# Gate-and-up chunks of a two-layer hybrid block: all four sums in one bank pool, read halfway by ScalarE, with other buffers and other priorities

## The chip, the cores and the metric

The kernel runs on one core of one Trainium2 chip. The metric is the device time of one execution in microseconds (us); lower is better. A time is the median of several runs of the same compiled program. Beside these runs stands one execution taken by the hardware profiler, and all rows shown below come from it.

## The reference, cut to what matters

Two layers run over 256 tokens of width 2048, all in float32. Each layer has a mixer (a state-space part and a latent attention), a cross-attention to 256 memory rows, and a feed-forward part. The change bears most on the last of these, and on what lies just before it:

```python
for l in range(DEPTH):                                   # DEPTH = 2
    ...
    x = x + mixed                                        # mixer, then @ w_out[l]
    ...
    x = x + memory_cross_attention(h, m, ...)            # ends in @ w_xo[l]
    h = rms_norm(x, ffn_norm_g[l])
    x = x + swiglu(h, w_gate[l], w_up[l], w_down[l])

def swiglu(h, w_gate, w_up, w_down):                     # w_gate, w_up: 2048 x 5632; w_down: 5632 x 2048
    return (jax.nn.silu(h @ w_gate) * (h @ w_up)) @ w_down
```

## The kernel before, in words

**Products in three parts.** A float32 product is made of three products of the rounded type float32r. Each unit of weights (256 rows by 512 columns, 512 KB, named `raw`) is split into `hi` (a cast, on ScalarE, ACT in the rows) and `lo` (raw minus hi, on VectorE, DVE). TensorE (PE) then multiplies hi by both parts of the activations and lo by the upper part. So every unit costs one cast on ACT, one subtraction on DVE and 6 matmuls (12 where both halves of the tokens take it).

**The feed-forward part.** The 5632 hidden columns go in 11 chunks of 512. Chunk 0 is done plainly. Chunks 1 to 10 go through `gate_up`, a seven-product scheme after Strassen for three quarters of the 2048 rows, with plain products (`x1`) for the rest. For it, `seven_rows` makes once per layer the split blocks a11, a12, a22, a21 of x and four sums s1 to s4 of them (the tiles `x7`, whose sums lie in `xs`; in the rows their splits are named `x<-xg,x` for a and `x<-xs,x` for s). The weights are summed on the fly by `add` on DVE (rows `raw<-raw,raw`): per chunk b11, b12, b22, b21 are pairs of 256-row units, and h11, h12, h22, h21 are single units that belong to the half blocks. Four sums are gathered in PSUM banks: `q`, `f` (from the pool acc, 4 banks) and `cg`, `cu` (from the pool tp, 4 banks). `q` is read three times while it goes on growing. The results meet in `uu` and `gg`; `gg` is then turned by a DMA transpose (`turn`: halves `hs`, turned `ht`, both in b4) and split into hTh and hTl for the down product. Chunks go in sections [0], [1,2], [3,4] and so on. After each chunk of a section come half of the four column blocks of the down product of the section before (`down`, each adds its two banks to x by `add_x`), so after chunks 1 and 2 it is 48 matmuls each, and after the later ones 96.

**What sets the order.** The program is first recorded and then put in order by a planner (`Recorder.issue`). It gives each engine, again and again, the operation that can start first by the planner's own costs, and of several with the same start the one with the lowest priority number: the place in the record plus `rec.bias`. `split_w` records its splits with -400, `add` its sums with -425, everything else in the feed-forward part with 0. The order on every engine and on the DMA queue of SyncE (SP) is then fixed, and each engine works through its own in that order.

**Buffers.** `b4` has 22 buffers of 4 KB per partition, `w` has 20 (raw, hi and lo of all weights), `s2` has 6 of 2 KB, acc and tp have 4 banks each. An operation that needs a buffer while `ahead` tiles recorded before it are still without one may take it only if more than min(margin, ahead) buffers are free; the margins stand in the last call of the kernel: b4 6, s2 2, tp 0, w 99, acc 4. `load_unit` asks for weights up to three units ahead, in the order of the list `ahead`.

Of the kernel before, what the change touches and what calls it, by code (L numbers as in the profile page):

```python
# [8 lines left out]
F32 = mybir.dt.float32  # L9
# [8 lines left out]
P = 128  # L18
S = 256
# [358 lines left out]
def hybrid_kernel(ctx: ExitStack, tc: tile.TileContext, const, vec, rows, x_in, x_tr, mem, mem_tr, positions, w_in, w_q_b,  # L378
# [110 lines left out]
    def load_unit(w, r0, c0, n, pieces=1):  # L489

        if not ahead and not asked:
            return ask(w, r0, c0, n, pieces)
        key = id(w), r0, c0
        while key not in asked or (ahead and len(asked) <= 2):
            first = ahead.pop(0)
            asked[id(first[0]), first[1], first[2]] = ask(*first, 512)
        return asked.pop(key)

    def load_raw(w, r0, c0, n, pieces=1):

        return [load_unit(w, r0 + 256 * h, c0, n, pieces) for h in range(2)]

    def ask(w, r0, c0, n, pieces=1):
        raw = wpool.tile([P, 2, n], F32, tag="w", name=nm("raw"), bufs=20)
        src = w[r0:r0 + 256, c0:c0 + n].rearrange("(k p) n -> p k n", p=P)
        for i in range(pieces):
            k = slice(2 // pieces * i, 2 // pieces * (i + 1))
            SP.dma_start(raw[:, k, :], src[:, k, :])
        return raw
# [116 lines left out]
    def norm_chunk_whole(j, ssx, g, by_dma=False):  # L626

        x_squares(j, ssx)
        xg = b4([P, 4, S], "xg")
        if by_dma:  # L630
            turn(lambda t: x[j][:, t, :], xg.rearrange("p b s -> p (b s)"))
            for b in range(4):
                copy(xg[:, b, :], xg[:, b, :], g[:, 4 * j + b:4 * j + b + 1])
            return xg
        for pair in range(2):
            ps = tp_tile().rearrange("p (b s) -> p b s", b=2)
            for i in range(2):
                b = 2 * pair + i
                for t in range(NT):
                    T.transpose(ps[:, i, t * P:(t + 1) * P], x[j][:, t, b * P:(b + 1) * P], ident)  # L640
                copy(xg[:, b, :], ps[:, i, :], g[:, 4 * j + b:4 * j + b + 1])
        return xg

    def seven_rows(xa, xb, n):


        a = {f"a{t + 1}{i + 1}": src[:, :, t * P:(t + 1) * P] for i, src in enumerate((xa, xb)) for t in range(NT)}
        if n == 4:
            sums = [b4([P, 2, 4, P], "xs") for _ in range(2)]
            tmp = [sums[i // 2][:, i % 2] for i in range(4)]  # L650
        else:
            sums = b4([P, 4, 2, P], "xs")
            tmp = [sums[:, i] for i in range(4)]
        out, room = {}, []
        for name in ("a11", "a12", "a22", "a21", "s1", "s2", "s3", "s4"):
            if name[0] == "s":
                a[name] = tmp[int(name[1]) - 1]
                do, u, v = {"s1": (V.tensor_sub, "a21", "a22"), "s2": (V.tensor_sub, "s1", "a11"),
                            "s3": (V.tensor_sub, "a11", "a21"), "s4": (V.tensor_add, "a12", "s2")}[name]
                do(a[name], a[u], a[v])  # L660
            if n == 4:
                d = b4([P, 2, 4, P], "x7", F32R)
            else:
                if not room:
                    both = b4([P, 2, 2, 2, P], "x7", F32R)
                    room = [both[:, 0], both[:, 1]]
                d = room.pop(0)
            copy(d[:, 0], a[name])
            V.tensor_sub(d[:, 1], a[name], d[:, 0].bitcast(F32))
            out[name] = d  # L670
        return out

    def load_T(src, j, g, name, pieces=1):
# [486 lines left out]
    def mem_T(l):  # L1160
# [10 lines left out]
        rec.after = None  # L1171
        return mT

    def add_x(j, accs):
        for t in range(NT):
            xs = x[j][:, t, :]
            V.tensor_add(xs, xs, accs[t])

    mixer_end, hidden_end = [None], [None]

# [120 lines left out]
            src = w[r0 + 256 * h:r0 + 256 * (h + 1), c0:c0 + 512].rearrange("(k p) n -> p k n", p=P)  # L1301
            G.dma_start(raw[h], src, accum_op=ALU.add)

    def add(out, a, b, do=V.tensor_add):
        rec.bias -= 425
        for o, u, v in zip(out, a, b) if isinstance(out, list) else [(out, a, b)]:
            do(o, u, v)
        rec.bias += 425

    def gate_up(wg, wu, c, x1, half, full, rstd):  # L1310

        c0 = 512 * c
        q, f = acc_tile(), acc_tile()
        cg, cu = tp_tile(), tp_tile()
        gg, uu = b4([P, NT, 512], "gg"), [s2([P, 512], "uu") for _ in range(NT)]  # L1320

        def product(acc, d, raw, start=False, stop=False):
            parts = split_w(raw)
            order = [(h, k, i) for h in range(len(parts)) for k, i in ((0, 1), (1, 1), (0, 0), (0, 2), (1, 0), (1, 2))]
            for m, (h, k, i) in enumerate(order):
                T.matmul(acc, d[:, i // 2, 2 * h + k, :], parts[h][i % 2][:, k, :], start=start and m == 0,
                         stop=stop and m == len(order) - 1, skip_group_check=True)

        b11 = load_raw(wg, 1024, c0, 512)
        product(q, full["a11"], b11, start=True)  # L1330
        h11 = load_unit(wg, 0, c0, 512)
        product(q, half["a11"], [h11])
        A.copy(gg[:, 0, :], q)

        b12 = load_raw(wu, 1024, c0, 512)
        add(b11, b11, b12)
        product(f, full["s1"], b11, start=True)
        h12 = load_unit(wu, 0, c0, 512)
        add(h11, h11, h12)
        product(f, half["s1"], [h11])  # L1340
        A.copy(uu[0], f)

        b22 = load_raw(wu, 1536, c0, 512)
        add(b11, b11, b22)
        add(b12, b12, b22)
        product(cu, full["s4"], b22, start=True)
        h22 = load_unit(wu, 256, c0, 512)
        add(h11, h11, h22)
        add(h12, h12, h22)
        product(cu, half["s4"], [h22])  # L1350
        product(q, full["s2"], b11)
        plus(b11, wg, 1536, c0)
        product(q, half["s2"], [h11])
        add(uu[0], uu[0], q, V.tensor_sub)

        b21 = load_raw(wg, 1536, c0, 512)
        product(cg, full["a12"], b21, start=True)
        h21 = load_unit(wg, 256, c0, 512)
        add(h11, h11, h21)
        product(cg, half["a12"], [h21])  # L1360
        product(q, full["s3"], b12)
        product(q, half["s3"], [h12])
        mm_chunk([cu, f], x1, load_w(wu, 512, c0, 512), 512, [False] * NT, [True, True], again=True)
        A.copy(uu[1], f)
        add(uu[1], uu[1], q, V.tensor_sub)
        add(uu[0], uu[0], cu)
        mm_chunk([cg, q], x1, load_w(wg, 512, c0, 512), 512, [False] * NT, [True, False], again=True)
        add(gg[:, 0, :], gg[:, 0, :], cg)
        A.activation(gg[:, 0, :], gg[:, 0, :], AF.Silu, scale=rstd[:, 0:1])

        product(q, full["a22"], b11)
        product(q, half["a22"], [h11], stop=True)
        A.activation(gg[:, 1, :], q, AF.Silu, scale=rstd[:, 1:2])
        for t in range(NT):
            V.scalar_tensor_tensor(gg[:, t, :], uu[t], rstd[:, t:t + 1], gg[:, t, :], op0=ALU.mult, op1=ALU.mult)
        return gg

    def ffn(l, xT, rstd):
# [19 lines left out]
        for sec in sections:  # L1398
            for i, c in enumerate(sec):
                if c == 0:  # L1400
                    ahead.extend((w, r + h, 0) for w in (wg, wu) for r in FULL for h in (0, 256))
                else:
                    ahead.extend((w, r, 512 * c) for w, r in (
                        (wg, 1024), (wg, 1280), (wg, 0), (wu, 1024), (wu, 1280), (wu, 0), (wu, 1536), (wu, 1792),
                        (wu, 256), (wg, 1536), (wg, 1792), (wg, 256), (wu, 512), (wu, 768), (wg, 512), (wg, 768)))
                if before:
                    n = DC // len(sec)
                    ahead.extend((wd, 512 * r + h, 512 * j) for j in range(n * i, n * (i + 1)) for r in before
                                 for h in (0, 256))
# [3 lines left out]
        for sec in sections:  # L1413
            hT = []
            for i, c in enumerate(sec):
                if c == 0:
                    xs = [lambda i, k, t: half[f"a{t + 1}{1 + k // 2}"][:, i, k % 2, :], x1]
                    xs += [lambda i, k, t, b=b: full[f"a{t + 1}{b}"][:, i, k, :] for b in (1, 2)]
                    ag = gemm(xs, wg, FULL, 0, 512)
                    hh = b4([P, NT, 512], "gg")  # L1420
                    for t in range(NT):
                        A.activation(hh[:, t, :], ag[t], AF.Silu, scale=rstd[:, t:t + 1])
                    au = gemm(xs, wu, FULL, 0, 512)
                    for t in range(NT):
                        V.scalar_tensor_tensor(hh[:, t, :], au[t], rstd[:, t:t + 1], hh[:, t, :], op0=ALU.mult,
                                               op1=ALU.mult)
                else:
                    hh = gate_up(wg, wu, c, x1, half, full, rstd)
                hc = chunk_T("hT")
                split_T_dma(hc, lambda t: hh[:, t, :], None, hh.rearrange("p t (u s) -> p (t u) s", s=S), (A, V))  # L1430
                hT.append(hc)
                if before:
                    n = DC // len(sec)
# [88 lines left out]
```

## Time and profile before

| | |
|---|---|
| median of 3 runs | 2263.99 us (2261.82 to 2264.88) |
| profiled execution, device time | 2267.05 us |
| its span, first to last instruction | 2265.3 us |
| mean granted TensorE clock | 0.997 of full speed |
| PE busy, share of the span | 98% |
| DVE busy | 84% |
| ACT busy | 66% |
| DMA, mean rate | 215 GB/s |

The profiled execution is 3.06 us longer than the median of the runs, and 1.75 us of its time lie outside the span. Matmuls follow one another in a pipeline, so a busy PE need not be a PE at its peak; the gaps of PE are what a change of order can win, since the number of matmuls stays.

### The profile page before, as it was taken

To read this page: it belongs to the slowest core of one execution; us is meant where nothing else is said; L and a number is where in the kernel's file an instruction comes from. 1 tells how busy PE (TensorE), PEld (TensorE's weight loads), DVE (VectorE), ACT (ScalarE), POOL (GpSimd) and SP (SyncE) were. 2 spreads that over 40 slices of the span, in tenths; PEclk is the share of its full clock that TensorE was granted. 3 is DMA by queue.
4 is the path that set the end of the run, shared out by engine and by line. 5 is a ranking of instruction groups with operands and counts; after the bars stand their busy time and mean duration, and the time that the engine had idled before them with its cause. 6 is when DMAs were issued, how large, how long until landed. Compare 5 with 4: busy or idle time off the path is not lost.

```text
span 2265.3 us, 29133 instructions
## 1 busy us (share of the span) xinstructions
PE 2222.9 (98%) x10118; PEld 1845.7 (81%) x10118; DVE 1910.6 (84%) x2568; ACT 1500.4 (66%) x2183; POOL 93.0 (4%) x78
## 2 busy tenths in 40 slices
PE   9999999998999999999999999999989999999999
PEld 9878878787888888888898788887878888888787
DVE  7898876789998999999778888857899999999894
ACT  7768666766766666676666686657666667666762
POOL 0001000000000000000000010000000000000000
PEclk9999999999999999999999999999999999999999
DMA  9866496676777777787777665856767777777773
GB/s 319 236 193 186 142 284 196 187 212 197 239 224 212 229 232 235 228 247 226 194 230 223 172 177 171 244 185 182 219 201 226 232 220 213 236 231 226 239 234 138
DMA packets 374515, 487.96 MB, mean 215 GB/s; under 512 B 145376, under 2 KB 168544, under 8 KB 374368
## 3 DMA queue, kind: packets, MB, share of 16 engines
q1 hardware_dynamic: 363456, 465.13, 65.1%
q0 software_dynamic: 10912, 20.98, 5.5%
q8 instruction: 79, 1.29, 0.2%
q14 instruction: 68, 0.56, 0.1%
HBM read 450.92 MB, written 2.10 MB: 200 GB/s over the span
## 4 chain that ended last, share of the span: by engine, by line
PE 71%; DVE 6%; DMA 5%; issue 2%; ACT 1%; SPq 0%; DVEq 0%; ACTq 0%
PE acc L374 59%; PE tp L374 13%; DVE lo L374 3%; DMA raw<-in_w_up_dram 1%; DVE raw L374 1%; DMA ht<-hs 1%; ACT hi L374 1%; DVE x L374 1%; DMA raw<-in_w_xv_dram 0%; DMA raw<-in_w_out_dram 0%; DMA raw<-in_w_in_dram 0%; DVE uu L374 0%; DMA raw<-in_w_gate_dram 0%; SPq L374 0%; DVE hTl L374 0%
## 5 line engine op out<-in xcount | busy, mean ns | idle before, releaser
L374 ACT CAST hi<-raw 128x1024 fp32r<-128x1024 f32 (+3 forms) x996 | 1002.7, 1034 | 559.9 <-PE acc L374 223.4
L374 DVE TENSOR_TENSOR lo<-raw,hi 128x1024 fp32r<-128x1024 f32 (+3 forms) x998 | 1167.9, 1200 | 177.3 <-ACT hi L374 125.2
L374 PE MATMUL acc<-hi,x 128*128 128x512 f32 x1392 | 373.1, 392 | 0.0
L374 PEld LDWEIGHTS acc<-hi,x 128*128 128x128 f32 x1392 | 263.4, 189 | 55.4
L374 PE MATMUL acc<-hi,xTh 128*128 128x512 f32 (+1 forms) x768 | 289.3, 377 | 0.0
L374 PE MATMUL acc<-hi,xTl 128*128 128x512 f32 (+1 forms) x768 | 289.1, 376 | 0.0
L374 DVE TENSOR_TENSOR raw<-raw,raw 128x1024 f32<-128x1024 f32 x200 | 239.2, 1221 | 50.7 <-DMA raw<-in_w_up_dram 50.2
L374 PE MATMUL acc<-hi,hTh 128*128 128x512 f32 x704 | 273.9, 389 | 0.0
L374 PE MATMUL acc<-hi,hTl 128*128 128x512 f32 x704 | 273.9, 389 | 0.0
L374 PE MATMUL acc<-lo,x 128*128 128x512 f32 x696 | 214.8, 394 | 13.2 <-DVE x L374 13.2
L374 PE MATMUL acc<-lo,xTh 128*128 128x512 f32 (+1 forms) x768 | 211.7, 378 | 6.0 <-DVE uu L374 4.2
L374 PE MATMUL acc<-lo,hTh 128*128 128x512 f32 x704 | 191.2, 390 | 1.3 <-DVE lo L374 1.3
L374 PEld LDWEIGHTS acc<-lo,xTh 128*128 128x128 f32 x768 | 140.6, 188 | 31.3 <-DVE uu L374 6.8
L374 PEld LDWEIGHTS acc<-lo,x 128*128 128x128 f32 x696 | 131.1, 190 | 42.5 <-DVE x L374 14.9
L374 PEld LDWEIGHTS acc<-hi,xTh 128*128 128x128 f32 x768 | 144.8, 189 | 23.2 <-issue 0.7
L374 PEld LDWEIGHTS acc<-hi,xTl 128*128 128x128 f32 x768 | 144.7, 188 | 23.1 <-issue 0.7
L374 PEld LDWEIGHTS acc<-lo,hTh 128*128 128x128 f32 x704 | 131.8, 188 | 30.1 <-DVE lo L374 3.0
L374 PEld LDWEIGHTS acc<-hi,hTh 128*128 128x128 f32 x704 | 132.1, 188 | 27.5
L374 PEld LDWEIGHTS acc<-hi,hTl 128*128 128x128 f32 x704 | 132.1, 188 | 27.4
L374 PE MATMUL tp<-hi,x 128*128 128x512 f32 x480 | 128.6, 390 | 0.0
L374 DVE TENSOR_TENSOR x<-x,acc 128x512 f32<-128x512 f32 x128 | 83.5, 682 | 32.5 <-PE acc L374 32.4
L374 PEld LDWEIGHTS tp<-hi,x 128*128 128x128 f32 x480 | 90.1, 188 | 19.2
(306 smaller groups left out, 2781.7 us busy)
## 6 DMA issues: line engine op xcount, KB each, us to landing
raw<-in_w_gate_dram SPq DMA_DIRECT2D x176, 512.0 KB, 4.9
raw<-in_w_up_dram SPq DMA_DIRECT2D x176, 512.0 KB, 4.5
raw<-in_w_down_dram SPq DMA_DIRECT2D x176, 512.0 KB, 5.4
raw<-in_w_in_dram SPq DMA_DIRECT2D x80, 512.0 KB, 4.4
raw<-in_w_out_dram SPq DMA_DIRECT2D x64, 512.0 KB, 4.5
raw<-in_w_gate_dram POOLq DMA_DIRECT2D x40, 512.0 KB, 7.5
raw<-in_w_in_dram SPq DMA_DIRECT2D x46, 368.0 KB, 4.5
raw<-in_w_kv_b_dram SPq DMA_DIRECT2D x16, 512.0 KB, 3.9
```

The costliest lines, as they stand in the source:

```text
L374: fn(*args, **kw)
```

## The change

It has these parts.

1. In `gate_up` the four sums q, f, cg, cu all come from tp; acc is left to the plain products and `down`.
2. ACT copies `q` to uu where it copied `f` before, and DVE subtracts that copy from `f`, where it subtracted `q` in its bank from a copy of `f`. For the second row block the copy of q now stands ahead of the plain product into cu and f.
3. `gg` and the chunk-0 `hh` are two half tiles in s2 in place of one b4 tile; the turned rows get a b4 tile of their own (`whole`).
4. From chunk 1 on, h11 and h12 (the units with row 0 in the list) are loaded to b4 in place of w.
5. The products of b22 and h22 into cu are recorded ahead of the sums that use b22 and h22.
6. In `seven_rows` the four sums s1 to s4 and their splits are recorded with 300 added.
7. `add_x` goes through `add`, so it has -425 in all its places.
8. In `norm_chunk_whole` the four transposes of a pair stand ahead of the two scaled copies out of their bank.

```diff
     def load_unit(w, r0, c0, n, pieces=1):
...
-            asked[id(first[0]), first[1], first[2]] = ask(*first, 512)
+            asked[id(first[0]), first[1], first[2]] = ask(*first[:3], 512, 1, first[3:])
...
-    def ask(w, r0, c0, n, pieces=1):
-        raw = wpool.tile([P, 2, n], F32, tag="w", name=nm("raw"), bufs=20)
+    def ask(w, r0, c0, n, pieces=1, other=False):
+        raw = b4([P, 2, n], "raw") if other else wpool.tile([P, 2, n], F32, tag="w", name=nm("raw"), bufs=20)
...
                     T.transpose(ps[:, i, t * P:(t + 1) * P], x[j][:, t, b * P:(b + 1) * P], ident)
+            for i in range(2):
+                b = 2 * pair + i
                 copy(xg[:, b, :], ps[:, i, :], g[:, 4 * j + b:4 * j + b + 1])
...
         for name in ("a11", "a12", "a22", "a21", "s1", "s2", "s3", "s4"):
+            if name == "s1":
+                rec.bias += 300
...
+        rec.bias -= 300
         return out
...
+    def add(out, a, b, do=V.tensor_add):
+        rec.bias -= 425
+        for o, u, v in zip(out, a, b) if isinstance(out, list) else [(out, a, b)]:
+            do(o, u, v)
+        rec.bias += 425
+
     def add_x(j, accs):
         for t in range(NT):
             xs = x[j][:, t, :]
-            V.tensor_add(xs, xs, accs[t])
+            add(xs, xs, accs[t])
...
-        q, f = acc_tile(), acc_tile()
-        cg, cu = tp_tile(), tp_tile()
-        gg, uu = b4([P, NT, 512], "gg"), [s2([P, 512], "uu") for _ in range(NT)]
+        q, f, cg, cu = (tp_tile() for _ in range(4))
+        gg, uu = [[s2([P, 512], n) for _ in range(NT)] for n in ("gg", "uu")]
...
         product(f, half["s1"], [h11])
-        A.copy(uu[0], f)
 
         b22 = load_raw(wu, 1536, c0, 512)
+        product(cu, full["s4"], b22, start=True)
         add(b11, b11, b22)
         add(b12, b12, b22)
-        product(cu, full["s4"], b22, start=True)
         h22 = load_unit(wu, 256, c0, 512)
+        product(cu, half["s4"], [h22])
         add(h11, h11, h22)
         add(h12, h12, h22)
-        product(cu, half["s4"], [h22])
         product(q, full["s2"], b11)
         plus(b11, wg, 1536, c0)
         product(q, half["s2"], [h11])
-        add(uu[0], uu[0], q, V.tensor_sub)
+        A.copy(uu[0], q)
+        add(uu[0], f, uu[0], V.tensor_sub)
...
         product(q, half["s3"], [h12])
+        A.copy(uu[1], q)
         mm_chunk([cu, f], x1, load_w(wu, 512, c0, 512), 512, [False] * NT, [True, True], again=True)
-        A.copy(uu[1], f)
-        add(uu[1], uu[1], q, V.tensor_sub)
+        add(uu[1], f, uu[1], V.tensor_sub)
         add(uu[0], uu[0], cu)
         mm_chunk([cg, q], x1, load_w(wg, 512, c0, 512), 512, [False] * NT, [True, False], again=True)
...
-                    ahead.extend((w, r, 512 * c) for w, r in (
+                    ahead.extend((w, r, 512 * c) + ((1,) if r == 0 else ()) for w, r in (
...
-                split_T_dma(hc, lambda t: hh[:, t, :], None, hh.rearrange("p t (u s) -> p (t u) s", s=S), (A, V))
+                split_T_dma(hc, lambda t: hh[t], None, None, (A, V))
```

## Rows read from the trace of the kernel before

**Rows 1.** The page's first part: busy time, share of the span, instructions.
```profile
PE   2222.9 (98%) x10118; PEld 1845.7 (81%) x10118; DVE 1910.6 (84%) x2568; ACT 1500.4 (66%) x2183; POOL 93.0 (4%) x78
```

**Rows 2.** Waits of PE, whole span: in total, times, longest (us).
```profile
PE acc L374 <- DVE x L374: 13.2, 4, 5.7
PE tp L374 <- DVE x L374: 5.2, 4, 2.3
PE tp L374 <- DVE lo L374: 4.8, 7, 1.2
PE acc L374 <- DVE uu L374: 4.2, 6, 1.3
PE acc L374 <- DVE lo L374: 3.1, 4, 1.8
```

**Rows 3.** Windows around chunk 2's start, both layers: busy (instructions); clock, DMA share, GB/s.
```profile
519.00:531.00 12.00, 12.00 (x55) 9.94 (x54) 11.00 (x11) 4.60 (x5) 0.00 (x0) 1.00 0.57 187
531.00:543.00 12.00, 6.36 (x17) 4.69 (x16) 8.14 (x11) 4.27 (x6) 0.00 (x0) 0.72 0.37 92
...
1658.00:1670.00 12.00, 6.29 (x19) 4.72 (x18) 8.49 (x12) 4.53 (x7) 0.00 (x0) 0.72 0.35 93
```

**Rows 4.** Timeline of DVE and PE around the first of these gaps.
```profile
529.48 2.36 DVE L374 TENSOR_TENSOR raw<-raw,raw 128x1024 f32<-128x1024 f32 x2
531.75 0.75 DVE L374 SCALAR_TENSOR_TENSOR gg<-uu,rx_y,gg 128x512 f32<-128x512 f32 x1
...
535.82 0.75 DVE L374 SCALAR_TENSOR_TENSOR gg<-uu,rx_y,gg 128x512 f32<-128x512 f32 x1
536.48 2.48 DVE L374 TENSOR_TENSOR x<-x,acc 128x512 f32<-128x512 f32 x4
...
537.22 1.22 PE L374 MATMUL acc<-lo,x 128*128 128x512 f32 x2 [5.64 <-DVE x L374]
```

**Rows 5.** Windows of longer stretches, columns as in rows 3 (PE, PEld, DVE, ACT, POOL).
```profile
481.00:620.00 139.00, 131.85 (x567) 107.53 (x566) 131.01 (x125) 99.57 (x111) 7.29 (x6) 0.98 0.77 228
...
1608.00:1750.00 142.00, 133.64 (x576) 108.91 (x574) 133.69 (x127) 101.04 (x112) 7.29 (x6) 0.98 0.76 228
...
560.00:620.00 60.00, 59.66 (x263) 49.03 (x263) 57.59 (x55) 43.29 (x48) 2.40 (x2) 1.00 0.79 242
...
860.00:920.00 60.00, 59.47 (x261) 48.61 (x260) 54.86 (x53) 41.67 (x45) 2.42 (x2) 1.00 0.72 226
...
457.00:481.00 24.00, 24.00 (x107) 19.87 (x107) 15.05 (x15) 9.39 (x10) 1.71 (x1) 1.00 0.47 153
```

**Rows 6.** Timeline of DVE and PE in chunk 5: the wait on uu.
```profile
747.37 1.22 DVE L374 TENSOR_TENSOR hTl<-gg,hTh 128x1024 fp32r<-128x1024 f32 x1
748.51 0.68 DVE L374 TENSOR_TENSOR uu<-uu,acc 128x512 f32<-128x512 f32 x1
...
749.24 0.73 PE L374 MATMUL acc<-lo,xTh 128*128 128x512 f32 x2 [0.61 <-DVE uu L374]
```

**Rows 7.** Timeline of DVE and PE after the mixer's output product, layer 0.
```profile
332.32 2.36 DVE L374 TENSOR_TENSOR lo<-raw,hi 128x1024 fp32r<-128x1024 f32 x2
334.60 1.27 DVE L374 SCALAR_TENSOR_TENSOR mTl<-mT,vecs,mTh 128x256 fp32r<-128x256 f32 x3
335.78 1.28 DVE L374 TENSOR_TENSOR x<-x,acc 128x512 f32<-128x512 f32 x2
...
336.52 0.44 PE L374 MATMUL tp<-cst,x 128*128 128x128 f32 x2 [2.26 <-DVE x L374]
```

**Rows 8.** DVE groups from 425 to 465 us: busy us, mean ns.
```profile
L374 DVE TENSOR_TENSOR x<-xs,x 128x256 fp32r<-128x256 f32 (+1 forms) x8 | 4.2, 555 | 0.0
```

**Rows 9.** Timeline of ACT and SP: chunk 1's rows are turned.
```profile
536.60 1.14 ACT L374 COPY hs<-gg 128x512 uint16<-128x512 uint16 x2 [2.93 <-DVE gg L374]
...
538.93 3.70 SPq L374 DMA_TRANSPOSE ht<-hs  x1
```

**Rows 10.** The page's last part: DMA issues, count, size, median us to landing.
```profile
raw<-in_w_up_dram SPq DMA_DIRECT2D x176, 512.0 KB, 4.5
...
ht<-hs SPq DMA_TRANSPOSE x63, 4.9
```

**Rows 11.** The page's costliest groups: busy us, mean ns, idle before and its releaser.
```profile
L374 ACT CAST hi<-raw 128x1024 fp32r<-128x1024 f32 (+3 forms) x996 | 1002.7, 1034 | 559.9 <-PE acc L374 223.4
L374 DVE TENSOR_TENSOR lo<-raw,hi 128x1024 fp32r<-128x1024 f32 (+3 forms) x998 | 1167.9, 1200 | 177.3 <-ACT hi L374 125.2
...
L374 DVE TENSOR_TENSOR raw<-raw,raw 128x1024 f32<-128x1024 f32 x200 | 239.2, 1221 | 50.7 <-DMA raw<-in_w_up_dram 50.2
```

More of the change, by code (lines that the diff above doesn't have):

```diff
@@ L1302, in plus @@
             G.dma_start(raw[h], src, accum_op=ALU.add)
[L1304 to L1308, printed above, removed]
     def gate_up(wg, wu, c, x1, half, full, rstd):
         c0 = 512 * c
-        q, f = acc_tile(), acc_tile()
-        cg, cu = tp_tile(), tp_tile()
-        gg, uu = b4([P, NT, 512], "gg"), [s2([P, 512], "uu") for _ in range(NT)]
+        q, f, cg, cu = (tp_tile() for _ in range(4))
+        gg, uu = [[s2([P, 512], n) for _ in range(NT)] for n in ("gg", "uu")]
         def product(acc, d, raw, start=False, stop=False):
@@ L1332, in gate_up @@
         product(q, half["a11"], [h11])
-        A.copy(gg[:, 0, :], q)
+        A.copy(gg[0], q)
         b12 = load_raw(wu, 1024, c0, 512)
@@ L1362, in gate_up @@
         product(q, half["s3"], [h12])
+        A.copy(uu[1], q)
         mm_chunk([cu, f], x1, load_w(wu, 512, c0, 512), 512, [False] * NT, [True, True], again=True)
-        A.copy(uu[1], f)
-        add(uu[1], uu[1], q, V.tensor_sub)
+        add(uu[1], f, uu[1], V.tensor_sub)
         add(uu[0], uu[0], cu)
         mm_chunk([cg, q], x1, load_w(wg, 512, c0, 512), 512, [False] * NT, [True, False], again=True)
-        add(gg[:, 0, :], gg[:, 0, :], cg)
-        A.activation(gg[:, 0, :], gg[:, 0, :], AF.Silu, scale=rstd[:, 0:1])
+        add(gg[0], gg[0], cg)
+        A.activation(gg[0], gg[0], AF.Silu, scale=rstd[:, 0:1])
         product(q, full["a22"], b11)
         product(q, half["a22"], [h11], stop=True)
-        A.activation(gg[:, 1, :], q, AF.Silu, scale=rstd[:, 1:2])
+        A.activation(gg[1], q, AF.Silu, scale=rstd[:, 1:2])
         for t in range(NT):
-            V.scalar_tensor_tensor(gg[:, t, :], uu[t], rstd[:, t:t + 1], gg[:, t, :], op0=ALU.mult, op1=ALU.mult)
+            V.scalar_tensor_tensor(gg[t], uu[t], rstd[:, t:t + 1], gg[t], op0=ALU.mult, op1=ALU.mult)
         return gg
@@ L1419, in ffn @@
                     ag = gemm(xs, wg, FULL, 0, 512)
-                    hh = b4([P, NT, 512], "gg")
+                    hh = [s2([P, 512], "gg") for _ in range(NT)]
                     for t in range(NT):
-                        A.activation(hh[:, t, :], ag[t], AF.Silu, scale=rstd[:, t:t + 1])
+                        A.activation(hh[t], ag[t], AF.Silu, scale=rstd[:, t:t + 1])
                     au = gemm(xs, wu, FULL, 0, 512)
                     for t in range(NT):
-                        V.scalar_tensor_tensor(hh[:, t, :], au[t], rstd[:, t:t + 1], hh[:, t, :], op0=ALU.mult,
+                        V.scalar_tensor_tensor(hh[t], au[t], rstd[:, t:t + 1], hh[t], op0=ALU.mult,
                                                op1=ALU.mult)
```

## The prediction, made before the changed kernel ran

> **What bounds the kernel now.** I read the page's busy times first: PE is busy 2222.9 of 2265.3 us and DVE 1910.6 [rows 1]. The change takes no matmul away, so all that it can win is PE's idle time (2265.3 - 2222.9 = 42.4 us) and time at a lower clock. The second view is the list of PE's waits [rows 2]. Its five largest lines come to 30.5 us, and all name DVE: 13.2 us in which a bank of acc waits for `add_x` (rows name it x), 5.2 us in which a transpose waits for the same addition, 4.8 and 3.1 us for `lo`, 4.2 us for `uu`. So PE sets the end, and it is DVE that makes it stop.
>
> The third view is the windows around the two largest of these waits, 5.6 to 5.7 us each, one per layer, where chunk 2 begins [rows 3]. In a stretch of 12 us without a wait there are 55 matmuls, 12 / 55 = 0.218 us each. In the 12 us with the wait there are 17 in layer 0 and 19 in layer 1, so 38 and 36 are missing: 8.3 and 7.9 us, together 16.1 us. That is more than the waits themselves (13.2 in all four): the mean granted clock of these stretches is 0.72, where it is 1.00 before. After the stop, then, PE ran part of the time at 1.2 GHz. The timeline says why it stopped: chunk 2's first bank in acc comes free only with the `x` additions at 536.48, and DVE had put weight sums, a `lo` and the two `gg` products ahead of them, though the sums were not yet wanted [rows 4].
>
> The fourth view says how much of this can be had. In 481 to 620 us, which holds chunks 1 and 2, DVE is busy 131.01 of 139 us, in layer 1 133.69 of 142 [rows 5]. Later it is looser: 54.86 of 60.
>
> **The change part by part.**
>
> Banks from one pool and `add_x` early (parts 1 and 7). Chunk 2 no longer needs a bank of acc, and the additions no longer queue behind weights. Either alone would undo the wait. Removed: 16.1 us, and the rest of the acc waits, 13.2 - 5.6 - 5.7 = 1.9 us. But DVE's work in these stretches stays: 139 - 131.01 + 142 - 133.69 = 16.3 us is the ceiling, since no stretch can be shorter than its DVE work. Its densest row, 57.59 of 60, is 96%; at that share both take (131.01 + 133.69) / 0.96 = 275.7 us in place of 281, a gain of 5.3 us. Ends 5.3 and 16.3. I take 10, near the middle, because the two w buffers that part 4 sets free let DVE work further ahead than before. What is late next: `lo` at chunk starts, as in the 4.8 and 3.1 us of [rows 2].
>
> ACT reads q (part 2). One copy and one DVE subtraction per half, as before, so no work is added. Before, the plain product into q had to wait until DVE had subtracted q from its bank; in chunk 5 that stood behind an `hTl` and held PE for 0.61 us [rows 6]. After, ACT copies q ahead of 24 plain matmuls (24 x 0.218 = 5.2 us), which cover it even behind several casts of 1.03 us [rows 11]. Gain: the whole 4.2 us of [rows 2], all of it in the later, looser chunks; lower end 0, if ACT has five casts in front.
>
> `add_x` ahead of the transposes (part 7 outside the feed-forward part). In layer 0 the additions of x waited behind two `lo` and three products for memory rows, 3.6 us of DVE work, and PE waited 2.26 us [rows 7]. With -425 they go first. I take 4 of the 5.2 us; ends 0 and 5.2. The price is that a `lo` of 1.20 us [rows 11] may start 0.68 us later behind an addition; DVE's work in sum is the same.
>
> Sums of x later (part 6). Four sums per call and their splits, 2 calls per layer: the splits take 4.2 us [rows 8], the sums at most about as much, so 8.4 us per layer move out of a dense stretch. Their cover is chunk 0: DVE idles 24 - 15.05 = 8.95 us in 457 to 481 [rows 5]. That just holds them, and they are first wanted in chunk 1. I take 0. Without the cover chunk 1's first s1 product waits, up to 8.4 us per layer; no wait before chunk 0 would be won, as [rows 2] has none that it cures.
>
> Transposes ahead of copies, and b22's product ahead of its sums (parts 8 and 5): the same instructions in another order, 0. What they could win lies in the 5.2 us above; what they could lose is bounded by the same, since no other wait of PE names transposes' banks.
>
> Other buffers (parts 3 and 4). Two units per chunk go from w to b4, `gg` goes out, a `whole` comes in. From the code, b4 holds 14 tiles through the whole feed-forward part (8 and 4 of x7, 2 of x1) and 2 of hT per finished chunk. When chunk 2 is to load there are 14 + 2, so 6 are free, and chunk 1's five tiles (hs, ht, whole, hTh, hTl) are recorded earlier. By the rule of the margins h11 may go at once (6 > 5), but h12 not before chunk 1's `hs` is free again. In the trace hs ends about 1.2 us after 536.60, and the transpose is issued at 538.93 [rows 9] and lands after 4.9 us [rows 10], at 543.8. Then h12 needs 4.5 us of DMA [rows 10], a sum of 1.22, a cast of 1.03 and a `lo` of 1.20 [rows 11]: 551.8. PE needs it after 30 matmuls of chunk 2 (6.5 us), which without the wait starts at 537.22 - 5.64 = 531.6 [rows 4], so at 538.1, and could be put off by the 12 matmuls of b22, to 540.7. If nothing moved up this is a wait of 11.1 us in each layer, as long as the one removed. But `gg` came late at 535.82 because weight sums were ahead of it [rows 4], and one of them is just the one that now can't start; and `hs` goes only with it. Before chunk 3 lie the same 48 down matmuls (10.5 us), from chunk 4 on 96 (21 us), and there I count the loads as late by about 1 us at most. Ends 0 and 22.2 plus about 1 us for each of 16 later starts; I take 3, nearer to none, since half of that chain is work that DVE had merely put off.
>
> Counter-rule: where a gap repeats on the engine that should be saturated, the Trainium skill (Perfetto Trace Analysis, Optimization Strategy) looks for too few SBUF or PSUM buffers for the next tile. For acc the trace agrees: chunk 2's wait has its twin in layer 1. By the same rule a b4 that is full at each chunk start would make a new repeating gap, and the sum would end above the time before (third rival).
>
> The sum: 10 + 4.2 + 4 - 3 = 15.2 us. The profiled execution's own time is 2265.3 + 1.75 outside the span = 2267.05, so 2251.9; it stands 3.06 above the median of the runs, so as a median 2248.8, say **2249 us**. With its terms' ends near their middle half the forecast's own range is 2240 to 2259.
>
> **The rivals.**
>
> All waits go. The two w buffers keep DVE ahead, and the stretches reach their ceiling: 16.3 + 4.2 + 5.2, and of the `lo` waits outside them 7.9 - 2 x 1.2 = 5.5: 31.2 us, 2233. For it: DVE idles even in the dense stretches. Against: it would have to work there without a pause. Chance 0.13.
>
> DVE gives it back. The order is better, but `lo` becomes the wait where chunks start, and the clock falls again there; 5.3 + 4.2 + 4 - 3 less the 8.4 us of late sums in one layer is 2, so 2262, and within 0.2%. For it: 96% in [rows 5]. Against: in 531 to 543 DVE itself was busy only 8.14 of 12, so the wait cost DVE time too. Chance 0.15. Here too belongs that the change doesn't act: the planner may order as before.
>
> Slower: h11 and h12 come late. Place: the first products of each `gate_up` that need h12. Price: 11.1 us at chunk 2 of each layer, with another (16.1 - 11.3) / 2 = 2.4 us of lower clock each time, 27 us, and about 1 us at later starts, 16 in all: 43 - 18.2 = 25 slower, 2289 at the worst; at half that, 2267 to 2270. It decides from the point where the mean over 20 chunk starts passes 18.2 / 20 = 0.9 us. For it: the chain of [rows 9, 10] is longer than the down product of chunk 1. Against: other products can fill in. Chance 0.20.
>
> **How the numbers follow.** The forecast has 0.52. What a measurement of this kernel can tell from no change is about 0.2%, 4.5 us: 2259.5 to 2268.5. Faster: 0.52 + 0.13 = 0.65; same: 0.15; slower: 0.20. The range goes from the first rival's 2232 to 2270, into the mild half of the last; about 0.05 is left out below and 0.12 above.
>
> **What the changed profile would show.** Right: no PE wait of over 2 us at chunk 2's start and a granted clock of 1.00 there; no line "acc waits for x" and none for uu; the transposes' wait for x under 2 us; DVE at 95% or more in chunks 1 and 2. Wrong: PE waits for `lo` or a `raw` sum at every chunk start, with a DMA into b4 behind `hs` or `whole` ahead of them; a wait at s1 in chunk 1 (late sums); or a wait on a copy of q by ACT.

## The result, and the profile after

The changed kernel takes 2237.86 us (median of 4 runs, 2235.69 to 2238.85) against 2263.92 (4 runs, 2261.82 to 2264.88): ratio 0.9885 [0.9868, 0.9902], 26.1 us faster. The forecast was 2249 with a range of its own of 2240 to 2259; the result lies just below that, inside 2232 to 2270, and nearer to the first rival's 2233. The span of the profiled execution went from 2265.3 to 2237.1 us, 28.2 less; about 2 us of this are the choice of executions, since the profiled one lay 3.06 us above the median before and 0.99 after.

The page's first part and the list of PE's waits, in us in total, times and longest, answer [rows 1, 2]:

```profile
PE 2215.1 (99%) x10118; PEld 1844.3 (82%) x10118; DVE 1918.6 (86%) x2576; ACT 1486.4 (66%) x2175; POOL 103.0 (5%) x78
...
PE tp L374 <- DVE lo L374: 5.5, 8, 1.3
PE acc L374 <- DVE lo L374: 2.6, 2, 2.5
PE tp L374 <- DVE x L374: 2.1, 1, 2.1
```

The lines "acc waits for x" (13.2 us) and "acc waits for uu" (4.2 us) are gone; the waits for `lo` stand almost as they were (8.1 us in place of 7.9).

The windows of the kernel after, with the columns of [rows 3, 5]. The last two lines answer to the two stretches of layer 0 in [rows 3]:

```profile
481.00:612.00 131.00, 129.64 (x568) 105.91 (x567) 128.21 (x124) 93.16 (x103) 7.29 (x6) 1.00 0.80 236
612.00:1090.00 478.00, 476.29 (x2098) 392.92 (x2097) 438.88 (x432) 317.37 (x351) 17.76 (x15) 1.00 0.76 232
1592.00:1726.00 134.00, 131.48 (x575) 107.31 (x574) 130.09 (x126) 95.23 (x106) 7.29 (x6) 1.00 0.79 235
1726.00:2200.00 474.00, 472.93 (x2083) 390.14 (x2082) 434.02 (x415) 314.94 (x345) 16.85 (x14) 1.00 0.75 231
519.00:531.00 12.00, 12.00 (x55) 9.94 (x54) 11.89 (x13) 5.95 (x7) 0.00 (x0) 1.00 0.51 175
531.00:543.00 12.00, 12.00 (x55) 9.94 (x54) 12.00 (x13) 8.71 (x9) 0.00 (x0) 1.00 0.68 219
```

Where 17 matmuls ran at a clock of 0.72, 55 now run at 1.00. The 568 matmuls of 481 to 612 took 139 us before (567 in [rows 5]), and the 575 of layer 1 took 142 (576): 8 us off each, 16 us in all. What allowed it stands in the third busy column: DVE works 128.21 of 131 us, 98%, and 12.00 of 12 in the window that used to hold the wait.

The same four long stretches of the kernel before:

```profile
481.00:612.00 131.00, 123.85 (x532) 100.90 (x531) 123.16 (x118) 93.45 (x104) 7.29 (x6) 0.97 0.76 218
612.00:1090.00 478.00, 474.34 (x2083) 389.75 (x2082) 434.32 (x416) 318.21 (x347) 17.86 (x15) 1.00 0.75 232
1592.00:1726.00 134.00, 125.64 (x541) 102.27 (x540) 120.27 (x114) 83.65 (x95) 4.87 (x4) 0.97 0.69 206
1726.00:2200.00 474.00, 469.49 (x2060) 385.52 (x2059) 434.87 (x415) 319.22 (x348) 19.37 (x16) 1.00 0.75 231
```

Before, PE did 532 + 2083 + 541 + 2060 = 5216 matmuls in these 1217 us, after 5324. At 0.227 us each (the timeline below: seven starts from 530.74 to 532.33) the 108 more are 24.5 us. So 16.0 of the 28.2 us come from the dense stretches at chunks 1 to 3, 24.5 - 16.0 = 8.5 from the later chunks, and 3.7 from elsewhere. These lie between the two feed-forward parts, where PE does 19 matmuls more, some 4 us (before, then after); which part of the change brought them was not separated:

```profile
1090.00:1592.00 502.00, 495.12 (x2373) 416.45 (x2372) 386.40 (x712) 333.41 (x630) 17.78 (x11) 1.00 0.67 197
1090.00:1592.00 502.00, 498.64 (x2392) 420.41 (x2391) 392.03 (x705) 330.97 (x627) 23.16 (x11) 1.00 0.67 196
```

Timeline of DVE, then of PE, at chunk 2's start, which answers [rows 4]:

```profile
519.20 0.74 DVE L374 SCALAR_TENSOR_TENSOR gg<-uu,rx_y,gg 128x512 f32<-128x512 f32 x1
...
526.86 1.28 DVE L374 TENSOR_TENSOR x<-x,acc 128x512 f32<-128x512 f32 x2
...
532.61 1.28 DVE L374 TENSOR_TENSOR x<-x,acc 128x512 f32<-128x512 f32 x2
...
530.74 0.39 PE L374 MATMUL acc<-hi,hTh 128*128 128x512 f32 x1
...
532.33 0.39 PE L374 MATMUL acc<-hi,hTl 128*128 128x512 f32 x1
532.56 0.62 PE L374 MATMUL tp<-lo,x 128*128 128x512 f32 x2
```

Chunk 2's first product goes to tp and starts 0.23 us after the last of `down`. The second pair of additions, at 532.61, now comes after that start and holds nobody.

### The profile page after: what moved, and what is told of

Same layout as the page of the kernel before. It is cut to its first block, busy times and chain, and to the rows that moved or that the text cites. A ratio compares the mean times of both kernels' runs of the same rounds, so it can differ in the third digit from the quotient of the medians.

```text
span 2237.1 us, 29087 instructions
## 1 busy us (share of the span) xinstructions
PE 2215.1 (99%) x10118; PEld 1844.3 (82%) x10118; DVE 1918.6 (86%) x2576; ACT 1486.4 (66%) x2175; POOL 103.0 (5%) x78
## 4 chain that ended last, share of the span: by engine, by line
PE 78%; DMA 3%; DVE 2%; ACT 1%; issue 1%; SPq 0%; ACTq 0%; DVEq 0%
PE acc L374 42%; PE tp L374 36%; DVE lo L374 2%; DMA ht<-hs 1%; ACT hi L374 0%; DMA raw<-in_w_up_dram 0%; DVE raw L374 0%; ACT whole L374 0%; DMA raw<-in_w_xk_dram 0%; DMA raw<-in_w_out_dram 0%; DMA raw<-in_w_xv_dram 0%; DMA raw<-in_w_kv_b_dram 0%; DMA raw<-in_w_q_b_dram 0%; DVE x L374 0%; DVE mTl L374 0%
## 5 line engine op out<-in xcount | busy, mean ns | idle before, releaser
L374 DVE TENSOR_TENSOR lo<-raw,hi 128x1024 fp32r<-128x1024 f32 (+3 forms) x998 | 1166.4, 1199 | 166.2 <-ACT hi L374 118.0
L374 PE MATMUL tp<-hi,x 128*128 128x512 f32 x1680 | 448.3, 389 | 0.0
L374 PEld LDWEIGHTS tp<-hi,x 128*128 128x128 f32 x1680 | 315.4, 188 | 65.9
L374 PE MATMUL tp<-lo,x 128*128 128x512 f32 x840 | 260.0, 391 | 5.6 <-DVE lo L374 5.5
L374 DVE TENSOR_TENSOR raw<-raw,raw 128x1024 f32<-128x1024 f32 x200 | 239.0, 1219 | 23.8 <-DMA raw<-in_w_up_dram 23.7
L374 PE MATMUL acc<-hi,xTl 128*128 128x512 f32 (+1 forms) x608 | 226.5, 373 | 0.0
L374 PE MATMUL acc<-hi,xTh 128*128 128x512 f32 (+1 forms) x608 | 226.5, 373 | 0.0
L374 PEld LDWEIGHTS tp<-lo,x 128*128 128x128 f32 x840 | 156.1, 188 | 43.5 <-DVE lo L374 9.6
L374 PE MATMUL acc<-lo,xTh 128*128 128x512 f32 (+1 forms) x608 | 154.8, 375 | 2.6 <-DVE lo L374 2.6
L374 PEld LDWEIGHTS acc<-hi,xTh 128*128 128x128 f32 x608 | 114.9, 189 | 16.8 <-issue 0.7
L374 PEld LDWEIGHTS acc<-hi,xTl 128*128 128x128 f32 x608 | 114.8, 189 | 16.8 <-issue 0.7
L374 PE MATMUL tp<-hi,xTh 128*128 128x512 f32 x320 | 124.5, 389 | 0.0
L374 PE MATMUL tp<-hi,xTl 128*128 128x512 f32 x320 | 124.5, 389 | 0.0
```

The source lines that it names most:

```text
L374: fn(*args, **kw)
```

## The experiments

Two theories stood against each other: that the time is that of chunk 2's wait, so that either cure of it brings the gain; and that DVE has no time to spare, so that a cure alone is given back, and the room (parts 3 and 4) and the copy of q (part 2) decide.

The runs were made on three other chips, on each of which the kernel before took 2271 to 2272 us, so only the ratios to it are compared. The table has, for each kernel, PE's waits for `lo` (both banks), for `uu` by DVE, and for x; DVE's idle time ahead of the weight sums (`raw` from two raws) that a load ended; and the matmuls in the four long stretches above, summed. The stretches stand at fixed times, so a kernel that starts the feed-forward part a few us later loses some matmuls by that. All columns but the ratio come from one execution per kernel, and the executions of one kernel lie 3 to 9 us apart, so a difference of a few us between two rows shows little. PE's waits for ACT are not in the table: x5 has 4.1 us of them for `uu`, x6 4.0 and x2 2.5, so the 0 of x5 is a wait that has moved from DVE to ACT's copy.

| kernel | ratio to before | lo | uu | x | idle for loads | matmuls |
|---|---|---|---|---|---|---|
| before | 1 | 7.9 | 4.2 | 18.4 | 50.2 | 5216 |
| after | 0.9885 | 8.1 | 0 | 2.1 | 23.7 | 5324 |
| x1 before + 7 | 1.0005 | 17.8 | 7.7 | 2.1 | 52.5 | 5208 |
| x2 before + 1, 2 | 0.9967 | 16.8 | 0 | 6.4 | 49.2 | 5243 |
| x5 before + 3, 4 | 0.9990 | 8.3 | 0 | 16.2 | 35.3 | 5219 |
| x9 before + 1 to 4 | 0.9887 | 10.8 | 0 | 4.5 | 28.4 | 5300 |
| x3 after - 4 | 0.9949 | 14.5 | 0 | 3.2 | 43.1 | 5256 |
| x8 after - 2 | 0.9966 | 18.4 | 6.3 | 4.0 | 31.5 | 5227 |
| x4 after - 6 | 0.9873 | 7.7 | 0 | 1.5 | 25.2 | 5317 |
| x7 after - 7 | 0.9884 | 11.8 | 0 | 2.4 | 29.3 | 5306 |
| x6 after, w of 18 | 1.0046 | 21.3 | 0 | 2.5 | 23.2 | 5170 |
| x12 after, more in b4 | 1.0146 | 53.6 | 0 | 2.7 | 61.3 | 5017 |
| x10 before, less DVE | 0.9905 | 3.0 | 0 | 6.3 | 56.6 | 5314 |
| x11 x1, less DVE | 0.9867 | 6.9 | 0 | 3.8 | 44.4 | 5332 |

**x1: the kernel before with part 7 alone.**

```diff
         for t in range(NT):
             xs = x[j][:, t, :]
+            rec.bias -= 425
             V.tensor_add(xs, xs, accs[t])
+            rec.bias += 425
```

> The kernel before with part 7 alone (the additions of x go through with -425); banks, buffers and everything else as before. Theory A, the order on DVE was the whole of the 5.6 us wait: the additions go ahead of the weight sums, the first bank of chunk 2 is free in time, no wait for x of over 1 us at chunk 2 in either layer, and 10 to 17 us are gained: 2247 to 2254. Rival B, the bank is the cause and the additions can't come much earlier, since chunk 2 must have the very banks that down's first column block holds: the wait falls by under half, gain under 8 us, 2256 or more.

Ratio 1.0005 [0.9994, 1.0016]. The order alone does remove the wait: the additions come at 528.57, where they came at 536.48 [rows 4], and neither layer has the gap. The largest lines of its list of PE's waits:

```profile
PE tp L374 <- DVE lo L374: 11.6, 14, 1.7
PE acc L374 <- DVE uu L374: 7.7, 8, 1.6
PE acc L374 <- DVE lo L374: 6.2, 7, 2.0
```

And its first two windows:

```profile
481.00:612.00 131.00, 127.73 (x560) 104.21 (x558) 127.49 (x122) 91.76 (x100) 7.29 (x6) 1.00 0.79 230
612.00:1090.00 478.00, 469.02 (x2051) 383.48 (x2050) 430.58 (x413) 320.62 (x349) 17.88 (x15) 1.00 0.76 229
```

In the first stretch PE is 28 matmuls ahead of before, and in the next it does 32 fewer; layer 1 repeats it (569 for 541, then 2028 for 2060). The whole gain is given back, mostly as waits for `lo` and `uu`, together 25.5 us for 12.1. Theory A is right about the order and wrong about the time: the theory of the wait alone, with its 10 us or more, falls.

**x2: the kernel before with parts 1 and 2.**

```diff
-        q, f = acc_tile(), acc_tile()
-        cg, cu = tp_tile(), tp_tile()
+        q, f, cg, cu = (tp_tile() for _ in range(4))
...
-        A.copy(uu[0], f)
...
-        add(uu[0], uu[0], q, V.tensor_sub)
+        A.copy(uu[0], q)
+        add(uu[0], f, uu[0], V.tensor_sub)
...
```

> The kernel before with parts 1 and 2 alone: q, f, cg, cu from tp, and q copied by ACT. Additions of x, buffers and all else as before. Theory A: the wait for a bank of acc can't occur at chunk 2, however late the additions are, and the waits for uu go as well: gain 14 to 21 us, 2243 to 2250. Rival B (DVE gives it back without the two w buffers): lo waits of 1 us or more at chunk starts in their place, gain under 10 us, 2254 or more.

Ratio 0.9967 [0.9949, 0.9986]. The other cure for the same wait; it too works, and most of it comes back as 14.2 us in which products into tp wait for `lo`, for 4.8 before. The two longest now stand at chunk 3's start, 3.2 us in layer 0 and 4.3 in layer 1:

```profile
PE tp L374 <- DVE lo L374: 14.2, 13, 4.3
```

**x5: the kernel before with parts 3 and 4**, `gg` and `hh` in s2, `whole` of its own, h11 and h12 in b4 (the diff of these parts above).

> The kernel before with parts 3 and 4 alone (gg and hh in s2, whole its own, h11 and h12 in b4); banks, reading of q, orders and additions as before. Theory A (room in w keeps DVE ahead, on its own account): the wait for x at chunk 2 stays as it was, about 16 us in both layers, but waits for lo and uu elsewhere fall; 4 to 8 us faster than before, ratio 0.9965 to 0.998. Rival B (room is worth something only once the wait at chunk 2 is gone, since that wait itself lets DVE catch up): ratio 0.999 to 1.001. Rival C (h12 comes late behind hs): slower, 1.002 or more.

Ratio 0.9990 [0.9978, 1.0001]. Chunk 2's wait stands (11.9 us, two times), so the buffers alone are worth nothing that can be told.

**x9: the kernel before with parts 1 to 4.**

> The kernel before with parts 1 to 4 together (banks, reading of q, buffers), without 5 to 8. Theory A (the gain is of these parts together: banks take the wait away, the copy of q and the room let DVE keep up; parts 5 to 8 add nothing): as after, ratio 0.987 to 0.990. Rival B (the orders of 5 to 8 matter when all else is there, though 6 and 7 alone did not): ratio 0.991 or more.

Ratio 0.9887 [0.9872, 0.9902], the whole gain. The sum of x2 and x5 would have been 0.9957; together they give 2.6 times that.

**x3: the kernel after without part 4.**

```diff
-                    ahead.extend((w, r, 512 * c) + ((1,) if r == 0 else ()) for w, r in (
+                    ahead.extend((w, r, 512 * c) for w, r in (
```

> The kernel after without part 4: h11 and h12 are loaded to w again. Theory A (room in w lets DVE work ahead, which is why DVE gave so little back): DVE idles more in chunks 1 and 2 and PE waits for lo at chunk starts; 5 to 12 us slower than after, 2243 to 2250. Rival B (the prediction's own term: h12 comes late behind hs): 3 us faster than after, 2235. Rival C, neither matters: within 2 us of 2237.9.

Ratio 0.9949 [0.9930, 0.9968], 0.0064 or some 14 us worse than after, a little more than theory A's 5 to 12. The page's line of the weight sums, of x3 and then of after (count, busy us, mean ns, idle ahead of them and its releaser):

```profile
L374 DVE TENSOR_TENSOR raw<-raw,raw 128x1024 f32<-128x1024 f32 x200 | 240.3, 1220 | 43.5 <-DMA raw<-in_w_up_dram 43.1
```

```profile
L374 DVE TENSOR_TENSOR raw<-raw,raw 128x1024 f32<-128x1024 f32 x200 | 239.0, 1219 | 23.8 <-DMA raw<-in_w_up_dram 23.7
```

With part 4 DVE stands 19.4 us less ahead of sums whose unit has not landed. That is the part that lets DVE work on when the wait is out of the way.

**x8: the kernel after without part 2** (ACT copies f, DVE subtracts q from its bank).

> The kernel after without part 2: ACT copies f and DVE subtracts q in its bank, as before, with all four sums in tp. Theory A (part 2 is what removes the wait for uu, and by the price of the wait alone): 4 to 6 us slower than after, ratio 0.990 to 0.992, with a wait of PE for uu of 4 to 8 us. Rival B (PE fills that wait with other products, now that q's bank is in tp): ratio 0.988 to 0.989.

Ratio 0.9966 [0.9955, 0.9976], 0.0081 or some 18 us worse than after, where the two theories gave 4 to 6 and nothing. The waits for `uu` are back with 6.3 us, beside the 4.2 of [rows 2], but that is a third of the loss. The rest goes with `lo`. The first lines of x8's list of PE's waits:

```profile
PE tp L374 <- DVE lo L374: 16.0, 14, 2.7
PE tp L374 <- DVE uu L374: 6.3, 7, 2.5
```

Ahead of `lo` DVE waited 139.4 us for ACT's `hi` in x8 and 118.0 in after. Its timelines of DVE, of ACT and of PE near 610 us, in this order:

```profile
607.29 9.30 DVE L374 TENSOR_TENSOR lo<-raw,hi 128x1024 fp32r<-128x1024 f32 x8
616.51 0.74 DVE L374 SCALAR_TENSOR_TENSOR gg<-uu,rx_y,gg 128x512 f32<-128x512 f32 x1
...
614.28 1.05 ACT L374 CAST hi<-raw 128x1024 fp32r<-128x1024 f32 x1 [5.24 <-DVE lo L374]
...
614.23 0.74 PE L374 MATMUL tp<-lo,xTh 128*128 128x512 f32 x2 [2.66 <-DVE lo L374]
```

Eight splits in a row hold DVE for 9.30 us, ACT stands for 5.24 us for one of them, and PE for 2.66. That part 2 cures this is not shown. The kernel after has eleven splits in a row at the same place and no wait of PE behind them, and x9, which has part 2 and the whole gain, waits as long there (first a line of after, then one of x9; in layer 1 of x9 it is 2.90 us):

```profile
602.79 12.57 DVE L374 TENSOR_TENSOR lo<-raw,hi 128x1024 fp32r<-128x1024 f32 x11
...
607.27 1.19 PE L374 MATMUL tp<-lo,xTh 128*128 128x512 f32 x2 [2.72 <-DVE lo L374]
```

By which steps reading the other bank costs more than its own wait stays open.

**x4: the kernel after without part 6** (s1 to s4 at their old rank), and **x7: the kernel after without part 7** (`add_x` without -425).

> The kernel after without part 6: the sums of x and their splits with no 300 added. Theory A (they only move to where DVE idles, as the prediction has it): within 2 us of 2237.9. Rival B (the sums are what made the transposes of the third column block wait just before chunk 0, 1.3 us per layer, and they take DVE from the first chunk's weights): 2 to 5 us slower, 2240 to 2243, with that wait back at the end of the cross-attention. Rival C (late sums cost chunk 1): 2 to 5 us faster.

> The kernel after without part 7 (additions of x with no -425). Theory A (with the sums in tp nothing waits for a bank of acc in time that hurts; the additions' place is free): ratio 0.988 to 0.9895, as after. Rival B (down's own banks run short, and transposes wait for x again): waits for x of 3 us or more in sum, ratio 0.990 to 0.993.

0.9873 [0.9852, 0.9894] and 0.9884 [0.9867, 0.9902]: both as after. With x9 this says that parts 5 to 8 are worth nothing that can be told here.

**x6: the kernel after with 18 buffers of w.** The two buffers that part 4 sets free are taken away again.

```diff
-        raw = b4([P, 2, n], "raw") if other else wpool.tile([P, 2, n], F32, tag="w", name=nm("raw"), bufs=20)
+        raw = b4([P, 2, n], "raw") if other else wpool.tile([P, 2, n], F32, tag="w", name=nm("raw"), bufs=18)
...
-            hi = wpool.tile([P, 2, n], F32R, tag="w", name=nm("hi"), bufs=20)
-            lo = wpool.tile([P, 2, n], F32R, tag="w", name=nm("lo"), bufs=20)
+            hi = wpool.tile([P, 2, n], F32R, tag="w", name=nm("hi"), bufs=18)
+            lo = wpool.tile([P, 2, n], F32R, tag="w", name=nm("lo"), bufs=18)
```

> The kernel after with 18 buffers in w in place of 20: h11 and h12 stay in b4, but the room that they left is taken away, so w holds what it held for the other units before. Theory A (it is the room that counts): as x3_h_in_w, ratio 0.994 to 0.997, with waits for lo at the starts of chunks 2, 3 and 4. Rival B (it is the order: units in b4 don't hold back the buffers of later units in w): as after, ratio 0.988 to 0.990.

Ratio 1.0046 [1.0031, 1.0061], slower than either theory had it, and slower than before. Room is worth much, but the run isn't clean: w serves the mixer and the attention too. Its span is 43.3 us longer than after's (some 7 of these are the other chip's, by the kernel before), and the four stretches hold (5324 - 5170) x 0.227 = 35.0 of them, so some 8 us lie outside the feed-forward part. DVE's idle time for loads stayed at 23.2 us, which suggests that that term goes by where h11 and h12 lie, and the waits for `lo` (21.3 us) by the room that is left in w.

**x12: the kernel after with h21 and h22 in b4 too.** The danger that the prediction priced, made larger: w has room for two more units, and b4, with its 22 buffers, holds two more.

```diff
-                    ahead.extend((w, r, 512 * c) + ((1,) if r == 0 else ()) for w, r in (
+                    ahead.extend((w, r, 512 * c) + ((1,) if r in (0, 256) else ()) for w, r in (
```

> The kernel after, with h21 and h22 in b4 too, so w has room for two more units for part of each chunk. Theory A (room in w counts, b4 has some left): 1 to 6 us faster than after, ratio 0.986 to 0.988. Rival B (b4 is full at chunk starts, these units come late, as the prediction feared of h12): 3 to 15 us slower than after, ratio 0.990 to 0.995, with waits for lo in the first products of chunks.

Ratio 1.0146 [1.0131, 1.0162], some 59 us worse than after, where rival B gave 3 to 15; the mean granted clock is 0.984 where after has 1.000. Its timelines of DVE, ACT, SP and PE in chunk 3, of which PE has done 72 matmuls by then, in order of time:

```profile
603.05 0.75 DVE L374 SCALAR_TENSOR_TENSOR gg<-uu,rx_y,gg 128x512 f32<-128x512 f32 x1
...
603.83 0.62 ACT L374 COPY hs<-gg 128x512 uint16<-128x512 uint16 x1 [1.29 <-DVE gg L374]
...
605.35 5.36 SPq L374 DMA_TRANSPOSE ht<-hs  x1
610.75 0.57 SPq L374 DMA_DIRECT2D raw<-in_w_up_dram  x1
...
612.73 2.52 ACT L374 COPY whole<-ht 128x1024 uint16<-128x1024 uint16 x2 [4.65 <-DMA ht<-hs]
...
614.96 2.36 DVE L374 TENSOR_TENSOR raw<-raw,raw 128x1024 f32<-128x1024 f32 x2 [9.69 <-DMA raw<-in_w_up_dram]
617.24 1.22 DVE L374 TENSOR_TENSOR lo<-raw,hi 128x1024 fp32r<-128x1024 f32 x1
...
618.51 1.22 PE L374 MATMUL tp<-lo,x 128*128 128x512 f32 x2 [12.98 <-DVE lo L374]
```

`gg`, `hs`, the transpose, and only behind it the load, then a sum, a `lo`, and PE: nearly the steps of the third rival, one chunk later, with 12.98 us for its 11.1, and at the same matmul of layer 1 another 12.05. One step differs. There the load waits until `hs` is free, after the turned rows land; here it goes out at 610.75, 2 us before they are read. So in the run it was its place behind the transpose on SP's queue that held it; why the planner put it there was not traced. By the Trainium skill (Perfetto Trace Analysis, Optimization Strategy) a gap that repeats on the engine that should be saturated can mean too few buffers for the next tile. In x12 the trace agrees: 18 waits for `lo` into tp, 51.8 us in all. But the gap of the kernel before repeated as well, and x1 closed it with no buffer added.

**x10: the kernel before with one sum left out, and x11: x1 with the same.** `b12 += b22` is left out: 40 DVE instructions (200 weight sums become 160), about 46 us of DVE's work, with the matmuls as they are.

```diff
-        add(b12, b12, b22)
```

> The kernel before, with one weight sum of each chunk left out (b12 += b22, two DVE instructions of 1.14 us per chunk, 40 in all, so the products of s3 and one output term are not the reference's). It is the base for the next run. DVE has 46 us less to do. Theory A (at chunk 2 DVE's order, not its load, holds the bank back, and elsewhere PE rarely waits): the waits for lo and uu fall, the wait for x at chunk 2 shrinks by the two sums in front of it or so; 6 to 14 us faster than before, ratio 0.994 to 0.9975. Rival B: no gain, 0.999 or more.

> The same sum left out of the kernel before with part 7 alone (x1_addx_only, which gained nothing with all its sums). Theory A (x1 lost its gain because DVE is the limit in chunks 1 to 3 and behind PE after them): with 46 us less for DVE the cure sticks, at least 10 us faster than x10_before_less_dve, ratio 0.988 to 0.992. Rival B (part 7 is harmful on its own account, by the places it takes from lo and uu, or by the planner's order): within 5 us of x10_before_less_dve.

0.9905 [0.9888, 0.9921] and 0.9867 [0.9852, 0.9881]. x10 alone gains more than its theory A had (6 to 14 us). With no priority or bank changed, acc's waits for x fell from 13.2 to 1.1 us, so DVE's load lay behind chunk 2's wait as well. (The edit also frees the splits of b12 from waiting for b22, so it takes away a little more than load.) With the load off, part 7 is worth 0.0038 (8.4 us by the medians) where it was worth -0.0005. That lies between the two expectations for x11, and the two traced executions, x10's the shortest of its four and x11's the longest, have the same span, 2243.0 and 2242.9 us. What the traces show is where part 7 still acts: in x10 acc waits in chunks 2 and 3 for ACT's `gg`, and in x11 that line is gone:

```profile
PE acc L374 <- ACT gg L374: 6.2, 4, 2.6
```

So the same cure seems to stick once DVE has time, by an amount that these runs leave open. The first two windows of x11, to be read against those of x1:

```profile
481.00:612.00 131.00, 130.05 (x574) 107.25 (x573) 124.87 (x119) 94.32 (x106) 7.29 (x6) 1.00 0.80 241
612.00:1090.00 478.00, 475.70 (x2093) 392.00 (x2092) 424.06 (x420) 318.10 (x349) 17.88 (x15) 1.00 0.77 232
```

DVE's 424.06 of 478 us stand beside 438.88 in after. In the second stretch PE does 2093 matmuls, x1's 2051.

## Why the prediction came out as it did

**Sign, place and ceiling: right.** PE is the bound and DVE makes it stop; the two large gaps with their low clock were the place; no wait of PE stands at chunk 2's start, the clock is 1.00 there, the lines for x in acc and for uu are gone, and DVE is at 98% where 95% was asked for. The one wait that misses its mark is the transposes' for x, 2.1 us against "under 2".

**The dense stretches, the term of parts 1 and 7: 16.0 us, not 10.** The forecast stood near the middle of 5.3 and 16.3; it came out at the upper end. It is not the work of these parts alone: without part 4 the two stretches win only 37 matmuls of the 70, 8.4 us (x3). The lower end rested on 57.59 of 60 us as the densest row before, and so as the share that DVE can reach [rows 5]. It was not the densest, as this row of the kernel before has 97%, by which the lower end would be 8.6:

```profile
481.00:532.00 51.00, 50.57 (x223) 41.17 (x221) 49.55 (x47) 37.02 (x41) 2.49 (x2) 1.00 0.80 238
```

Nor was either a limit: DVE did 98% over 131 us.

**"Either alone would undo the wait": true of the wait, false of the time.** x1 and x2 each undo it and bring 1.0005 and 0.9967. This is the second rival's mechanism, DVE giving it back as `lo`, and for either cure alone it is what happens. Parts 1 and 2 bring the whole gain with parts 3 and 4 beside them (x9). Part 1 without part 2, and part 7 with part 4, were not run on the kernel before.

**Part 4: the sign was wrong.** It was put down as -3 us for fear of h12 behind `hs`; taking it away costs some 14 us (x3). The chain is real, but at this fill of b4 it doesn't decide: PE waits for no late load at chunk 2 (the timeline above). With two more units in b4 a late load of nearly this kind decides (x12). The two free buffers of w were named in the prediction, as a reason to take 10 in the first term, and not given a price.

**Part 2: mis-sized.** 4.2 us was the wait that PE shows, and it went; without the part some 18 us go (x8). The later chunks, where the forecast put only these 4.2 us, won 8.5. The price was read from PE's waits for `uu` alone; most of the loss in x8 goes with waits for `lo`, 18.4 us for 8.1.

**Part 7 outside the feed-forward part: the wrong step.** 4 us were taken, and [rows 7] were its evidence. The same place after, DVE and then PE:

```profile
335.19 2.36 DVE L374 TENSOR_TENSOR lo<-raw,hi 128x1024 fp32r<-128x1024 f32 x2
337.47 1.27 DVE L374 SCALAR_TENSOR_TENSOR mTl<-mT,vecs,mTh 128x256 fp32r<-128x256 f32 x3
338.66 1.28 DVE L374 TENSOR_TENSOR x<-x,acc 128x512 f32<-128x512 f32 x2
...
339.39 0.44 PE L374 MATMUL tp<-cst,x 128*128 128x128 f32 x2 [2.14 <-DVE x L374]
```

The order is the same two `lo`, three products and then x, and the wait is 2.14 us for 2.26. The additions were not held behind those by rank there, and -425 moved nothing. The other waits of this line did go, 5.2 to 2.1, but they went in x7 too (2.4), without the part; in x9, without parts 5 to 8, 4.5 are left.

**Parts 5, 6 and 8 at nothing: right**, as far as 0.2% tells (x4, x9).

**The rivals.** The slower one is x12. "All waits go" named the reason rightly, two w buffers that keep DVE ahead, and came nearest in time; its 5.5 us of `lo` waits did not go (8.1 us are left), and the later chunks' 8.5 us stand in their place.

**The sum.** By place the forecast had 10 - 3 us for the chunk starts, 4.2 for the later chunks and 4 elsewhere; the profiles have 16.0, 8.5 and 3.7. That the last agrees is luck: it was put down to part 7, and x7 without it comes to the same time as after. The range of 2232 to 2270 held because it was drawn down to the first rival; the forecast's own missed by 2 us. One reading was a little short: 12 / 55 counts matmuls that only reach into the window, and at 0.227 us from start to start the 74 missing ones are 16.8 us, not 16.1.

**Open:** by which steps part 2 is worth four times its wait; what brought the 3.7 us between the feed-forward parts; and how the worth of part 4 divides between room in w and the place of h11 and h12, since x6 took room from other stages too.

## What to carry to other kernels

Where the engine behind the bound one has little time to spare (here DVE, 131.01 of 139 us and 434.32 of 478), undoing a wait may only move it: look for what that second engine itself stands for (here 50 us ahead of sums, for loads), and cure both together. An effect of parts is then not the sum of what each brings alone: here 0.9967 and 0.9990 alone, 0.9887 together. A cure by order and a cure by a buffer can both remove the same line from the list of waits, so the line's going is no proof of time won; count the work done over the next stretches too.

## What was not expected of the hardware

The prediction took 96% for the share of its time that DVE can work in a dense stretch; DVE then ran 12.00 of 12 us and 128.21 of 131 with its instructions at their old durations (`lo` 1199 ns in the mean, 1200 before). And one DMA transpose held SP's queue for 5.36 us in x12, with the load behind it issued at 610.75 and the data used at 614.96: a place on SP's queue was more than half of a wait of 9.69 us on DVE.
